# A list scheduler that models the port shared by VectorE and GpSimd, with new places for residual rows, projection weights and the first tiles, in a two-layer hybrid decoder trunk

## Chip, cores, metric

One Trainium2 chip at a time, all 8 cores (four on each of its two dies: cores 0 to 3 and 4 to 7), one sequence of the batch on each. The metric is device time in microseconds (us) of the slowest core. VectorE is written DVE, ScalarE ACT and GpSimd POOL where the profile does so; PE is TensorE and PEld its loading of weights. In profile lines L858 is line 858 of the kernel, `arena` the on-chip memory SBUF that holds all tiles, `ps` the accumulators in PSUM, `x244` a count of instructions; a group of instructions then shows busy us and the mean ns of one, and behind the bar the engine's idle time before them and what ended it.

An execution of an 8-core program is here either fast or slow. In a slow one some cores show a TensorE clock of 0.81 over part of the time and the run is some per cent longer. Only fast runs are compared, or, inside a slow run, the cores of a die whose clock was not touched.

## The reference, cut to what matters

```python
D_MODEL, BATCH, SEQ, DEPTH = 1024, 8, 4096, 2
D_FF, IN_WIDTH = 2816, 2560
# mixer A: 4 heads x 128 in chunks of 128; mixer B: 8 heads x 64, three dilated patterns

def reference(x, c, ada_w, ...):
    for l in range(DEPTH):
        mod = silu(c) @ ada_w[l] + ada_b[l]              # 9 rows of shift, scale, gate
        y = modulate(rmsnorm(h, norm_g[l, 0]), sh1, sc1)
        h = h + 0.5 * g1 * swiglu(y, ffn1_wg[l], ffn1_wu[l], ffn1_wd[l])
        y = modulate(rmsnorm(h, norm_g[l, 1]), sh2, sc2)
        u_a, v_a, q_b, k_b, v_b = split(y @ w_in[l])     # combined projection
        out_a = spatial_gating(u_a, v_a, ...)
        out_b = dilated_mixture(rope(q_b), rope(k_b), v_b)
        h = h + g2 * (concat(out_a, out_b) @ w_out[l])
        y = modulate(rmsnorm(h, norm_g[l, 2]), sh3, sc3)
        h = h + 0.5 * g3 * swiglu(y, ffn2_wg[l], ffn2_wu[l], ffn2_wd[l])
    return rmsnorm(h, final_g)
```

## The kernel before

The program is a graph of tasks. Each task names one or more engines that may do it, with a duration for each, and what it reads and writes. A list scheduler simulates the core, gives every task an engine and a place in that engine's order, and the result is emitted as instructions. A tile is 512 positions by 1024 channels; a core has eight of them. Cuts are marked `# ...`.

The scheduler. `r` is when a task can start; `m` is the later time from which TensorE may take it without risk of standing still. When several matmul chains are possible, TensorE prefers one whose `m` has passed. The other engines take the task with the smallest deadline `L`, whichever place it has in the task's list of engines.

```python
def schedule(self, bw=230.0, dlat=2300.0, dmargin=3000.0, cmargin=250.0, backlog=9000.0):
    # ...
    def release(t):
        r = m = 0.0
        if t.opts[0][0] == "pe":
            for _, ds, _, off in t.ins:
                for d in ds:
                    if d.eng == "pe":
                        continue
                    x = d.end - off
                    r = max(r, x)
                    m = max(m, x + (dmargin if d.dma else cmargin))
            # ...
        else:
            for d in t.deps:
                r = max(r, d.end)
            m = r
    # ...
    def pick(e, now):
        # ... TensorE: best by (t.mready <= now, -t.pos)
        for t in av:
            # ...
            k = t.L
            # ...
            if best is None or k < bk:
                best, bk = t, k
        return best, nxt
```

The norm of a tile and its engines, first choice first (the operation `nu` multiplies rows by the reciprocal root, `ny` applies scale and shift):

```python
def norm_sum(ht, pos):
    # ... ACT squares each of 8 row groups; they are added up
        G.op([pool(f, 1450), dve(f, 620)], reads=[ba, bq], writes=[bo], name="sqsum", pos=pos)
    # ... one matmul sums over the partitions ("nsum"), ACT: ln and exp

def norm_y(ht, slot, l, i, pos):
    # ...
        G.op([dve(f, 620), pool(f, 1450)], reads=[brs], writes=[bh], name="nu", pos=pos)
        # ...
        G.op([dve(g, 340), act(..., 705), pool(g, 1000)], reads=[bh, bm], writes=[by[kc]], name="ny", pos=pos)
```

Places: four activation slots `ACT[0..3]`, six gate-weight slots from `GU0`, three down-weight slots from `WD0`, one residual buffer `HB` that holds a whole tile for a norm, three small tiles for SwiGLU and a ring of four for residual rows:

```python
class FFN:
    def __init__(self, l, which, src, bsrc, nres=4):
        # ...
        self.res = Ring(steps(HR, 2048, nres), [128, T], F32, "hres")

def norm_load(t, src, bsrc, pos):
    ht = HT(HB)                       # always the same place
    load_h(ht, t, src, bsrc, pos)
    return ht

# start
cond(range(24), -3000.0, steps(ACT[3], 4096, 5) + steps(ACT[2], 4096, 5), WD0)   # modulation rows
for n, t in enumerate(range(4)):
    nrm(t, 0, -3000.0 + 1000.0 * n)
# ... first projection of a layer: all 20 weight blocks behind one another, from ACT[0]
mx0 = Mixer(l, ACT[0], ACT[2])
mx0.load(True, p2)
# ... end
for t in (4, 5):
    norm_out(norm_load(t, hS, bHS, s2), t, s2 + 20000.0 * (t - 4))
fc.downs((7,), ht)
norm_out(norm_load(6, hS, bHS, G.M), 6, G.M - 30000.0)
norm_out(ht, 7, G.M, True)

G.POOLS = {"ps": 8, "sg": 3}
```

The softmax here doesn't subtract the row's maximum and nothing guards it: scores larger than these inputs give would overflow.

## Time and profile before

| | before |
|---|---|
| median of 3 runs | 5174.43 us |
| the three runs | 5164.05, 5174.43 (fast), 5717.63 (slow) |
| profiled execution | slow: 5531.6 us on core 0 |
| matmuls per core | 26282 |
| busy us, core 0: PE / DVE / ACT / POOL | 5292.9 / 2923.6 / 1874.5 / 912.7 |

The busy PE of this table is stretched by the low clock, so its 96% says little about where a fast run stands still.

Every matmul got the time that it takes in an unbroken row at full clock (0.216 us for 512 columns, 0.056 or 0.05 us for the narrow ones, from the traces); they sum to 4741 us on a core. The *loss* of a stage is its length less that work. One figure is too high: the 2752 matmuls on 64 rows run in pairs, a pair every 56 ns in the trace, and 0.05 us each counts them almost twice. About 60 us of the 4741 are therefore not work (12 of them in the projection stages), the same in every kernel: differences stand, the losses themselves are too small by that much.

### The profile page before, as it was taken

The page shows a single profiled execution, that of the slowest core. Times are in us where ns is not written, and L with a number is a line of the kernel's source. Part 1 is how long each engine was busy: PE and PEld are TensorE (multiplying, and loading weights), DVE is VectorE, ACT ScalarE, POOL GpSimd, SP SyncE. Part 2 cuts the span into 40 slices and gives each one's busy share as a digit, 9 for nine tenths or more (in the row PEclk, how much of TensorE's full clock was granted, in tenths as well). Part 3 has the DMA queues.
Part 4 walks back from the last instruction along what each step waited for, and adds up shares of the span by engine and source line. Part 5 has one row for each costly group of instructions (what it writes and reads, how often), then busy time and mean ns, then how long its engine had stood idle before and what let it go on. Part 6 is the DMA issues. An engine that isn't in the chain of part 4 may idle for free.

```text
span 5531.6 us, 75923 instructions; the slowest of 8 cores (5456.8 to 5531.6 us)
## 1 busy us (share of the span) xinstructions
PE 5292.9 (96%) x26282; PEld 2385.5 (43%) x26282; DVE 2923.6 (53%) x4662; ACT 1874.5 (34%) x2715; POOL 912.7 (16%) x789
## 2 busy tenths in 40 slices
PE   3999989999999999999999999889999899999997
PEld 1344334444444444444444444344444454544443
DVE  6532387447277436445533333785554954556533
ACT  3210244435144433432122111454452544534311
POOL 2100143011143000120011001440112510012000
PEclk7788878887888888888889999999999999999998
DMA  7534756476746456565535117754756454465327
GB/s 238 145 84 112 214 154 158 107 193 184 176 161 175 123 146 182 153 207 156 159 113 190 39 39 227 191 164 129 200 143 197 152 174 149 129 183 185 115 67 253
DMA packets 389817, 866.37 MB, mean 157 GB/s; under 512 B 151456, under 2 KB 184608, under 8 KB 383264
## 3 DMA queue, kind: packets, MB, share of 16 engines
q1 hardware_dynamic: 371344, 773.02, 44.6%
q0 software_dynamic: 18096, 88.49, 10.0%
q8 instruction: 216, 3.54, 0.3%
q14 instruction: 161, 1.32, 0.1%
HBM read 760.59 MB, written 241.17 MB: 181 GB/s over the span
## 4 chain that ended last, share of the span: by engine, by line
PE 83%; DVE 7%; DMA 4%; issue 3%; ACT 2%; POOL 1%; DVEq 0%; SPq 0%; ACTq 0%; POOLq 0%
PE ps L905 46%; PE ps L932 21%; PE ps L1028 7%; PE ps L1331 4%; PE ps L1270 3%; PE ps L1247 2%; DVE arena L858 2%; DMA arena<-hS 1%; DVE arena L1088 1%; DVE arena L839 1%; DVE arena L1097 1%; DMA arena<-ada_w 1%; DMA arena<-xP 1%; DMA hS<-arena 1%; DVE arena L861 0%
## 5 line engine op out<-in xcount | busy, mean ns | idle before, releaser
L905 PE MATMUL ps<-arena 128*128 128x512 bf16 x11264 | 2783.7, 409 | 39.4 <-DVE arena L861 25.6
L905 PEld LDWEIGHTS ps<-arena 128*128 128x128 bf16 x11264 | 1135.3, 103 | 1503.7 <-issue 862.9
L932 PE MATMUL ps<-arena 128*128 128x512 bf16 x5632 | 1341.1, 403 | 14.0 <-DVE arena L936 9.3
L911 ACT ACTIVATE arena<-ps 128x512 f32<-128x512 f32 x704 | 420.0, 597 | 1483.0 <-PE ps L905 1463.0
L932 PEld LDWEIGHTS ps<-arena 128*128 128x128 bf16 x5632 | 572.5, 102 | 755.3 <-issue 356.2
L913 DVE SCALAR_TENSOR_TENSOR arena<-arena,ps 128x512 f32<-128x512 f32 x704 | 481.7, 685 | 784.9 <-ACT arena L911 783.6
L1028 PE MATMUL ps<-arena 128*128 128x512 bf16 x2560 | 643.7, 416 | 31.5 <-ACT arena L1079 10.2
L936 DVE SCALAR_TENSOR_TENSOR arena<-ps,arena 128x512 f32<-128x512 f32 x256 | 191.6, 750 | 887.0 <-PE ps L932 776.4
L918 DVE TENSOR_TENSOR arena<-ps,arena 128x512 bf16<-128x512 f32 x704 | 485.0, 690 | 277.3 <-PE ps L905 263.8
L832 ACT ACTIVATE arena<-arena 128x512 f32<-128x512 f32 x448 | 268.4, 625 | 914.4 <-DMA arena<-hS 564.5
L1253 ACT ACTIVATE arena<-ps 128x1024 bf16<-128x1024 f32 (+1 forms) x384 | 355.3, 933 | 379.6 <-PE ps L1247 379.1
L1028 PEld LDWEIGHTS ps<-arena 128*128 128x128 bf16 x2560 | 265.9, 105 | 387.2 <-issue 249.0
L839 POOL TENSOR_TENSOR arena<-arena 128x512 f32<-128x512 f32 (+1 forms) x150 | 200.7, 1338 | 993.8 <-ACT arena L832 574.9
L1256 DVE TENSOR_TENSOR arena<-arena 128x1024 bf16<-128x1024 bf16 (+1 forms) x384 | 248.7, 649 | 153.5 <-ACT arena L1253 150.8
L858 POOL TENSOR_TENSOR arena<-arena 128x512 f32<-128x512 f32 x140 | 219.8, 1588 | 387.9 <-ACT arena L846 381.1
L858 DVE TENSOR_TENSOR arena<-arena 128x512 f32<-128x512 f32 x244 | 252.7, 1076 | 28.9 <-ACT arena L846 26.7
L1331 PE MATMUL ps<-arena 128*128 128x512 bf16 x1024 | 253.2, 409 | 4.0 <-ACT arena L1110 2.2
L839 DVE TENSOR_TENSOR arena<-arena 128x512 f32<-128x512 f32 (+1 forms) x242 | 189.8, 784 | 106.7 <-ACT arena L832 73.5
L1270 PE MATMUL ps<-arena 128*128 128x128 bf16 x2736 | 225.4, 229 | 15.5 <-DVE arena L1256 14.8
L1270 PEld LDWEIGHTS ps<-arena 128*128 128x128 bf16 x2736 | 190.8, 103 | 105.8 <-issue 68.1
L1309 POOL TENSOR_TENSOR arena<-arena 64x512 bf16<-64x512 f32 x64 | 101.1, 1580 | 770.7 <-ACT arena L1304 738.9
L863 ACT ACTIVATE arena<-arena 128x512 bf16<-128x512 f32 x224 | 174.9, 808 | 141.7 <-DVE arena L858 123.5
(71 smaller groups left out, 2751.8 us busy)
## 6 DMA issues: line engine op xcount, KB each, us to landing
arena<-wguS SPq DMA_DIRECT2D x242, 512.0 KB, 4.4
arena<-hS SPq DMA_DIRECT2D x192, 512.0 KB, 6.2
arena<-wdS SPq DMA_DIRECT2D x128, 704.0 KB, 6.2
arena<-ada_w SPq DMA_DIRECT2D x144, 512.0 KB, 8.2
hS<-arena SPq DMA_DIRECT2D x248, 256.0 KB, 5.8
arena<-hS SPq DMA_DIRECT2D x184, 256.0 KB, 5.0
wguS<-wgu POOLq DMA_DIRECT2D x66, 512.0 KB, 7.5
hS<-arena SPq DMA_DIRECT2D x64, 512.0 KB, 4.9
```

The source lines that it names most:

```text
L832: G.op([act(lambda e, sq=sq, hk=hk: e.activation(out=sq, in_=hk, func=AF.Square), 520)], reads=[ht.b[kc]], writes=[bq], name="sq", pos=pos)
L839: f = lambda e, a=a, sq=sq, out=out: e.tensor_tensor(out=out, in0=a, in1=sq, op=ALU.add)
L858: f = lambda e, hk=hk: e.tensor_tensor(out=hk, in0=hk, in1=rs, op=ALU.mult)
L905: main([(lambda e, kc=kc, half=half, bk=bk, y=y, gu=gu: e.matmul(bank(bk), lhsT=gu[:, half, kc, :], rhs=y[:, kc, :], start=(kc == 0), stop ...
L911: G.op([act(lambda e, sg=sg, gb=gb: e.activation(out=sgv[sg.i], in_=bank(gb), func=AF.Tanh, scale=0.5), 490, "tanh")], reads=[gb], writes= ...
L913: G.op([dve(lambda e, sg=sg, gb=gb: e.scalar_tensor_tensor(out=sgv[sg.i], in0=sgv[sg.i], scalar=1.0, in1=bank(gb), op0=ALU.add, op1=ALU.mu ...
L918: G.op([dve(lambda e, sg=sg, ub=ub, o=o: e.tensor_tensor(out=o, in0=bank(ub), in1=sgv[sg.i], op=ALU.mult), 610)], reads=[ub, sg], writes=[ ...
L932: main([(lambda e, j=j: e.matmul(bank(bk), lhsT=wd[:, j, :], rhs=a[:, j, :], start=(j == 0), stop=(j == FC - 1)), [bwd, ba[j]], MM) for j ...
L1028: ins.append((lambda e, lhs=lhs, rhs=rhs, kc=kc: e.matmul(bank(bk), lhsT=lhs, rhs=rhs, start=(kc == 0), stop=(kc == KC - 1)), rd + [by[kc] ...
L1253: G.op([act(lambda e: e.activation(out=pv, in_=ps[:, sb.i:sb.i + 2, c0:512], func=AF.Exp, scale=0.125), 910 if anyprev else 490, "exp")], ...
L1270: return e.matmul(o, lhsT=v[:, vi, h * 64:h * 64 + 128], rhs=pT[:, h, pc, b, :], start=(pc == 0 or not prev), stop=(pc == 1))
L1331: main([(lambda e, kc=kc, m=m, bk=bk: e.matmul(bank(bk), lhsT=w[:, m, kc, :], rhs=mx[:, kc, :], start=(kc == 0), stop=(kc == KC - 1)), [bw ...
```

## The change

Its intent: let TensorE know which results are likely to be late, let the scheduler know that VectorE and GpSimd get in each other's way, give residual rows, attention reciprocals and SwiGLU tiles one common pool, put projection weights into gate slots that are free earlier, and give the first and last tiles places of their own. The core of the diff (about half left out, marked `...`; the dropped parts are the load rules, conversions and names):

```diff
-    def schedule(self, bw=230.0, dlat=2300.0, dmargin=3000.0, cmargin=250.0, backlog=9000.0):
+    def schedule(self, bw=300.0, dlat=2300.0, dmargin=3000.0, cmargin=250.0, backlog=9000.0):
...
+        port = [0.0]
...
-                        x = d.end - off
-                        r = max(r, x)
-                        m = max(m, x + (dmargin if d.dma else cmargin))
+                        r = max(r, d.end - off)
+                        m = max(m, d.late - off + cmargin)
...
                 for d in t.deps:
                     r = max(r, d.end)
-                m = r
+                    m = max(m, d.late)
...
+                if e != t.opts[0][0] and t.L > hp + 2500.0:
+                    nxt = min(nxt, now + 300.0)
+                    continue
...
+                if e == "dve" and port[0] > now and any(o[0] == e and o[3] == "x" for o in t.opts):
+                    k += 2.0 * (port[0] - now)
...
+            if e == "dve" and o[3] == "x" and free["pool"] > now and port[0] > now:
+                dur += min(port[0], free["pool"]) - now
+            if e == "pool" and not t.dma:
+                port[0] = now + dur
...
+                t.late = max(t.end, t.mready + dur + 2000.0) + dmargin
             else:
                 t.end = st + dur + LAT[e]
+                t.late = max(t.end, t.mready + o[2] + LAT[e] if e != "pe" else 0.0)
...
+        def dvex(fn, ns):
+
+            return ("dve", fn, ns, "x")
...
-                G.op([pool(f, 1450), dve(f, 620)], reads=[ba, bq], writes=[bo], name="sqsum", pos=pos)
+                G.op([pool(f, 1250), dvex(f, 615)], reads=[ba, bq], writes=[bo], name="sqsum", pos=pos)
...
-                G.op([dve(f, 620), pool(f, 1450)], reads=[brs], writes=[bh], name="nu", pos=pos)
+                G.op([dvex(f, 615), pool(f, 1300)], reads=[brs], writes=[bh], name="nu", pos=pos)
...
-                G.op([dve(g, 340), act(... 705), pool(g, 1000)],
+                G.op([act(... 725), dvex(g, 420), pool(g, 1500)],
...
-                    ap, b = self.res.take()
+                    b = Bank(1, "sm")
+                    ap = lambda: smv[b.i]
...
-        cond(range(24), -3000.0, steps(ACT[3], 4096, 5) + steps(ACT[2], 4096, 5), WD0)
+        cond(range(16), -3000.0, steps(WD0 + 4096, 4096, 3) + steps(ACT[0], 4096, 5), WD0, -26000.0)
...
-                for n, t in enumerate(range(4)):
-                    nrm(t, 0, -3000.0 + 1000.0 * n)
+                for t in range(4):
+                    nrm(t, 0, 3456.0 * t - 2500.0, None, (HB, ACT[1], ACT[2], ACT[3])[t])
...
-            mx0.load(True, p2)
+            for n, c in enumerate((1, 2, 3)):
+                mx0.load(c, GU0 + 8192 * n, True, p2)
+            for n, c in enumerate((0, 4)):
+                mx0.load(c, ACT[0] + 8192 * n, True, p2)
...
-                    norm_out(norm_load(t, hS, bHS, s2), t, s2 + 20000.0 * (t - 4))
+                    norm_out(norm_load(t, hS, bHS, s2, (GU0, HB)[t - 4]), t, s2 + 15000.0 * (t - 4))
...
-                norm_out(norm_load(6, hS, bHS, G.M), 6, G.M - 30000.0)
+                norm_out(norm_load(6, hS, bHS, G.M, GU0), 6, G.M - 25000.0)
...
-        G.POOLS = {"ps": 8, "sg": 3}
+        G.POOLS = {"ps": 8, "sm": 7}
```

An operation marked `"x"` (by `dvex`) is one on VectorE that the model lets wait until GpSimd is done. The rotary sums, the gatings, the attention normalisations and the v-norms got the same treatment as the norm lines shown.

## The prediction

> **What bounds the kernel now.** First the list of cores, because it decides how everything else is read. The profiled execution is a slow one (5533 us, while two of the three timed runs took 5164 and 5174). The clocks say why.
>
> ```profile
> core 0: 5531.6 us, clock 0.893
> core 3: 5522.7 us, clock 0.897
> ```
>
> Next the page: its engine row and the clock row of the core that it shows (core 0).
>
> ```profile
> PE 5292.9 (96%) x26282; PEld 2385.5 (43%) x26282; DVE 2923.6 (53%) x4662; ACT 1874.5 (34%) x2715; POOL 912.7 (16%) x789
> PEclk7788878887888888888889999999999999999998
> ```
>
> TensorE is busy for 96%, but up to about 2800 us its clock is 0.81. A slow TensorE hides the other engines' waits, so the idle time of that half is no measure of the fast state. Core 3 had the reverse: full clock first, 0.81 later. Both run the same program, so I joined their full-clock halves. These are busy times in stretches, core 0 first and then core 3; the number after the x is the matmuls done.
>
> ```profile
> 0.00:2815.00 2815.00, 2683.91 (x12296) 1165.43 (x12297) 1483.40 (x2395) 915.06 (x1315) 462.63 (x421) 0.81 0.58 160
> 2815.00:5532.00 2717.00, 2609.04 (x13988) 1220.08 (x13986) 1440.25 (x2267) 959.46 (x1400) 450.07 (x368) 0.98 0.51 153
> ...
> 0.00:2452.00 2452.00, 2247.30 (x12294) 1053.00 (x12295) 1474.98 (x2395) 908.62 (x1315) 464.76 (x421) 0.98 0.68 184
> ```
>
> Core 3 reaches matmul 12294 at 2452 us, core 0 at 2815. The joined execution takes 2452 + 2717 = 5169 us, which is the fast time (5164 and 5174). So I take the fast state to be this program without the 0.81 clock, and read every stage from whichever core ran it at full clock: first four rows core 3, last four core 0. Columns: stretch, its length, busy PE, PEld, DVE, ACT, POOL, clock, DMA share, GB/s.
>
> ```profile
> 0.00:160.00 160.00, 58.72 (x214) 22.34 (x215) 104.08 (x150) 61.33 (x85) 37.64 (x34) 0.84 0.77 220
> 480.00:800.00 320.00, 275.83 (x1246) 121.65 (x1245) 224.81 (x398) 127.67 (x198) 120.08 (x110) 0.95 0.72 197
> 800.00:1280.00 480.00, 457.51 (x2969) 224.22 (x2968) 292.27 (x473) 235.88 (x332) 74.32 (x66) 0.99 0.71 180
> 1280.00:1600.00 320.00, 288.73 (x1374) 130.42 (x1373) 215.80 (x387) 128.10 (x196) 127.96 (x104) 0.97 0.68 189
> ...
> 3400.00:3700.00 300.00, 263.93 (x1227) 116.94 (x1226) 225.65 (x396) 136.54 (x215) 134.05 (x114) 0.94 0.72 201
> 4150.00:4420.00 270.00, 246.90 (x1151) 111.35 (x1149) 187.65 (x346) 107.47 (x166) 109.00 (x85) 0.97 0.54 173
> 5380.00:5517.00 137.00, 119.94 (x540) 53.26 (x538) 48.47 (x64) 21.77 (x35) 9.54 (x7) 0.94 0.79 253
> 5517.00:5532.00 15.00, 0.59 (x1) 0.10 (x1) 8.86 (x14) 2.58 (x4) 0.00 (x0) 0.62 0.55 210
> ```
>
> I count a stage's loss as idle PE plus busy PE times (1 - clock), because matmuls after an idle stretch run at half clock. Start (0 to 160): 101 + 9 = 110 us. The four projection stages: 44 + 14 = 58, 31 + 9 = 40, 36 + 16 = 52 and 23 + 7 = 30, together 180. The end (from 5380): 31 + 8 = 39. The rest, mainly the attention stretches (800 to 1280 is 22 + 5 = 27), about 52. Sum 381 us. The floor that no schedule beats is therefore about 5169 - 381 = 4788 us, and the change can win only from those 381.
>
> **Why they are lost.** At the start (core 3's timeline), each of the four tiles' norms ends in a one-column-sum matmul (L842), and each waits for its own load.
>
> ```profile
> 46.67 0.59 PE L842 MATMUL ps<-arena 128*128 128x512 bf16 x1 [46.67 <-DVE arena L839]
> 75.03 0.58 PE L842 MATMUL ps<-arena 128*128 128x512 bf16 x1 [12.44 <-DVE arena L839]
> 86.26 1.44 PE L905 MATMUL ps<-arena 128*128 128x512 bf16 x3 [10.65 <-DVE arena L861]
> ```
>
> All four tiles share one residual buffer, so tile 1's load starts only at 54 us, when tile 0 is consumed. The end shows the same on core 0: a norm whose rows come late stands in front of ready matmuls.
>
> ```profile
> 5464.44 1.15 ACT L832 ACTIVATE arena<-arena 128x512 f32<-128x512 f32 x2 [18.01 <-DMA arena<-hS]
> 5475.92 0.59 PE L842 MATMUL ps<-arena 128*128 128x512 bf16 x1 [13.28 <-DVE arena L839]
> ```
>
> In the projection stages VectorE is 70 to 75% busy on average, but in bursts: counted by the program's own position marks, times the mean of each row below, 120 us of TensorE work at the first projection carry about 165 us of DVE work. Two groups are dear (core 0's groups by shape).
>
> ```profile
> L858 DVE TENSOR_TENSOR arena<-arena 128x512 f32<-128x512 f32 x244 | 252.7, 1076 | 28.9 <-ACT arena L846 26.7 <-DMA hS<-arena 2.0
> L1097 DVE TENSOR_TENSOR arena<-arena 128x512 bf16<-128x512 f32 x72 | 146.1, 2051 | 1.6 <-DVE arena L1088 1.4
> ```
>
> **What the Trainium skill says.** "SBUF - State Buffer", section "Who interferes with whom": a VectorE instruction with two SBUF inputs contends with a GpSimd instruction that reads SBUF, and whoever comes second is blocked outright. The trace agrees: of the 244 norm products (L858) on DVE, the 204 that overlapped a GpSimd operation took 1.15 us on average and the other 40 took 0.69; the SwiGLU product that reads PSUM (L913) took 0.68 either way. "TensorE: Matmul & The Clock Gate", section "What's actually happening": after an idle window of some 3.4 us the array falls to half clock, and a peak-current limiter may hold 13/16. The trace agrees on both: the clock record shows 0.50 around the stalls in stretches of 3 to 7 us, and 0.81 over half of each core's time. That page has the limiter act on a whole die; here cores 0, 1, 6 and 7 had it first and 2 to 5 later.
>
> **The change, part by part.** No arithmetic is added or removed; matmuls stay 26282. What differs is who does what, when, and where tiles lie. I compared the order of instructions of both programs on each engine.
>
> Start. Before: 16 modulation rows and 4 row loads (plus c), 21 transfers of 0.5 MB, precede the first product, which starts at 54 us; tile 1 follows only at 86. After: four tiles have four places, tile 0 and 1 load ahead of and among the 16 rows, tiles 2 and 3 right behind. That is 25 transfers before the first product, 4 more: at the roughly 320 GB/s that the DMA row shows from 11 to 44 us, 4 x 0.52 MB / 320 = 6.5 us later landing. But both norm sums are done by then, so only the modulation itself remains, and TensorE gets 32 products of two tiles, then a sum, 56 products, the last sum, and 1320 without a break (before 16, 48, 112, 1232). I put the first product at 52 to 58 us and another 8 to 12 us of gaps after it: loss 65 instead of 110, **-45 us**.
>
> Projection stages. Work leaves DVE: 46 rotary sums x 2.05 = 94 us, 86 square sums x 0.78 = 67, 69 modulations x 0.87 = 60, 23 attention normalisations x 1.04 = 24, 26 gatings x 0.84 = 22, 17 norm products x 1.08 = 18, 36 v-norms x 0.42 = 15; sum 300 us of 2924. GpSimd gets 85 + 115 + 39 + 36 + 27 - 33 - 7 = +262 us at its own means (1.85, 1.34, 1.50, 1.58, 1.59; modulations at 1.49 and v-norms at 0.71 leave it), ScalarE 91 x 0.81 + 46 x 0.48 = +96. By the position marks some 210 of the 300 us leave these four stages: the 165 us of DVE work per 120 us of TensorE become about 112. GpSimd stays at 84 of those 120 us (86 before), and rises by 27 or 28 us in each of the other three, to 138 in the busiest 180. DVE no longer exceeds TensorE, but is at 93% of it, so short waits stay. 12 of 20 projection weight loads go to gate slots and need not wait for the down products; the seven shared small tiles let residual rows be fetched earlier, which meets the 14 us that down products wait (9.3 on their residual sums). I let half of the 180 us go: **-90 us**.
>
> Attention stretches: the mask and SwiGLU orders hardly change: **-10 us**. End: tiles 4, 5 and 6 get other places than the single one, which meets the 13.3 us wait plus its cold clock and 3.1 us on a weight load; the last tile's tail (15 us after the last product) is unchanged: **-17 us**.
>
> Sum -162, so 5169 - 162 = 5007. GpSimd's longer row of work is in order and locks the port against 384 mask products and the 227 norm products left on DVE; I hold back 13 us for that: **5020 us**, 2.9% faster.
>
> **Rivals.** (a) GpSimd becomes the bound of the projection stages: it is the slowest at every operation that it gets (1.34 against 0.69), and its queue is in order. If it does, the 90 us shrink to 20 and the time is about 5090. For: the rotary sums already take 1.85 there. Against: it had 60% of those stretches free. (b) TensorE's new order waits for something else, such as the weight conversions now made in DRAM for the first down products, or loads packed more tightly; DMA is at 0.7 in these stages. Then 5080 to 5150. Against: DMA is at 0.5 or below in the gate stages where the conversions lie. (c) All losses but the start and end vanish: 4950 or less. Against: 93% DVE load leaves no room for that. (d) A fuller TensorE trips the 0.81 clock in runs that are fast now; then nothing of this shows, but such runs count as slow.
>
> **Range and chances.** The start and end (62 us) are the surest. To be over 2% faster than 5169 the time must be below 5066, that is 103 us: start, end and 41 of the 100 others. I give that 0.82, within 2% 0.16, slower 0.02. Range 4955 to 5095, from rival (c) to a little above rival (a).
>
> **What would show it.** The first long row of gate products should begin before 60 us and no gap above 8 us follow; DVE busy should fall to about 2600 to 2700 us and GpSimd rise to 1150 or more; the rotary sums on DVE should be near 26 and shorter than 2.05 us; the 13 us wait at the end gone; the losses of the four projection stages at full clock near 90. If GpSimd is above 80% busy there and matmuls wait on it, rival (a) was right; if DVE busy fell and the losses stayed, the waits were chains of latency and not load, and I was wrong in that step.

## The result, and the profile after

| | before | after |
|---|---|---|
| median, same chip | 5220.02 us (4 runs, 5164.05 to 5717.63, two of them slow) | 5043.77 us (4 runs, 5035.81 to 5560.87, one of them slow) |
| fast runs after | | 5035.81, 5041.85, 5045.69 |
| full-clock cores of all runs, mean (sd between cores) | 5153 us (11) | 5017 us (17) |

The ratio of fast runs is **0.9752** (95%: 0.9728 to 0.9775): faster, by 2.5%. Ratios here are the mean time of one kernel's fast runs over that of the other's of the same rounds, so not quite the ratio of the medians. "Full-clock cores" are all cores of all runs whose mean clock was 0.978 or more; this lets slow runs with one untouched die count too, and it is the yardstick of the experiments.

The list of cores of the kernel after. This execution is a fast one:

```profile
core 2: 5034.3 us, clock 0.987
core 6: 4988.7 us, clock 0.992
```

The page of the same execution (core 2):

```profile
PE 4797.4 (95%) x25784; PEld 2274.2 (45%) x26282; DVE 2739.8 (54%) x4359; ACT 1957.7 (39%) x2862; POOL 1147.0 (23%) x955
PEclk9999999999999999999999999999999999999999
```

The clock row (PEclk, the granted clock in tenths, in 40 slices) has no 7s and 8s any more, but that is the state of the run and not the change. (498 matmul records are missing on this core; cores 2 and 4 are therefore left out of the loss table.) DVE lost 184 busy us against the page of before, POOL gained 234, ACT 83.

The four projection stages on core 1, all at full clock (columns as in the prediction: stretch, its length, busy PE, PEld, DVE, ACT, POOL, clock, DMA share, GB/s):

```profile
522.00:837.00 315.00, 295.47 (x1586) 138.39 (x1585) 216.16 (x408) 177.06 (x275) 151.51 (x119) 0.95 0.61 167
1350.00:1608.00 258.00, 245.90 (x1439) 118.66 (x1438) 176.93 (x315) 130.53 (x193) 90.18 (x71) 0.98 0.59 170
2882.00:3296.00 414.00, 393.74 (x2035) 181.50 (x2033) 245.56 (x444) 195.56 (x303) 168.63 (x136) 0.98 0.67 188
3689.00:3968.00 279.00, 266.61 (x1314) 122.27 (x1313) 197.56 (x350) 147.02 (x224) 141.48 (x108) 0.98 0.64 193
```

DVE is busy for 836 of 1266 us, 66%. POOL is at most 51% busy (141 of 279). PE stands still for 64 us in the four.

Two groups of core 1 by shape, which answer to the dear ones of before (L858 is now L879, L1097 is L1121):

```profile
L879 DVE TENSOR_TENSOR arena<-arena 128x512 f32<-128x512 f32 x227 | 259.6, 1179 | 30.2 <-DMA hS<-arena 14.6 <-ACT arena L867 12.4 <-ACT arena L1081 3.1
L1121 POOL TENSOR_TENSOR arena<-arena 128x512 bf16<-128x512 f32 x102 | 201.4, 2055 | 85.5 <-DVE arena L1112 77.8 <-ACT arena L867 4.8 <-DMA qS<-arena 1.7
```

Of 128 rotary sums 102 are now on POOL (56 before), at 2.06 us each; the norm products left on DVE became longer, not shorter.

The start, TensorE's timeline of core 2:

```profile
46.09 0.59 PE L863 MATMUL ps<-arena 128*128 128x512 bf16 x1 [22.75 <-DVE arena L860]
62.82 10.10 PE L925 MATMUL ps<-arena 128*128 128x512 bf16 x32 [16.14 <-ACT arena L884]
74.51 0.38 PE L863 MATMUL ps<-arena 128*128 128x512 bf16 x1 [1.59 <-POOL arena L860]
```

Both norm sums are done at 47 us; then TensorE waits 16 us for the modulation (L884), and after that no gap on this core is longer than 2.5 us. Before, gaps of 12 and 11 us followed. Why the 16 us are so long, the timeline of core 1 shows:

```profile
27.09 12.24 POOL L879 TENSOR_TENSOR arena<-arena 128x512 f32<-128x512 f32 x6 [1.41 <-ACT arena L867]
29.88 2.27 DVE L756 SCALAR_TENSOR_TENSOR arena<-arena 128x1024 f32<-128x1024 f32 x1
38.15 2.27 DVE L756 SCALAR_TENSOR_TENSOR arena<-arena 128x1024 f32<-128x1024 f32 x1
40.35 1.21 DVE L756 SCALAR_TENSOR_TENSOR arena<-arena 128x1024 f32<-128x1024 f32 x1
```

L756 makes the modulation rows, L879 is the norm product. While POOL works through six norm products of tile 0 (27.09 to 39.33 us), a row takes DVE 2.27 us; the row that starts at 40.35, after them, takes 1.21. It is the same instruction on the same shape.

The end, first TensorE's timeline of core 2 and then its waits from 4900 us on:

```profile
4941.89 6.59 PE L953 MATMUL ps<-arena 128*128 128x512 bf16 x22 [3.88 <-DMA arena<-wdS]
5024.35 0.38 PE L863 MATMUL ps<-arena 128*128 128x512 bf16 x1 [3.13 <-POOL arena L860]
```

```profile
PE ps L953 <- DMA arena<-wdS: 10.2, 5, 3.9
```

The norm that stood in front of ready matmuls for 13.3 us is gone. In its place down products wait 10.2 us, in five pieces, for their own weights.

The loss by stage (us, mean of the cores at full clock with all records: 3 of the kernel before, run again in the first experiment, and 6 of the kernel after):

| stage | before | after | change | predicted |
|---|---|---|---|---|
| before the first matmul, and the first 60 us of work | 115.1 | 72.6 | -42.5 | -45 |
| four projection stages | 56.2 + 27.9 + 57.3 + 27.5 = 168.9 | 30.8 + 13.0 + 36.5 + 15.3 = 95.6 | -73.3 | -90 |
| attention, FFN and the rest | 95.5 | 71.5 | -24 | -10 |
| end (last 141 us of work) | 32.8 | 26.8 | -6.0 | -17 |
| held back | | | | +13 |
| sum | 412.2 | 266.5 | -146 | -149 |

The two cores left out of "after" are its two slowest, which makes this sum about 7 us too good (eight cores average 5014 us, these six 5008). Over all full-clock cores the mean moved from 5153 to 5017, by -136; the slowest core from 5169 to 5041, by -128, because the cores now lie further apart (sd 17 instead of 11).

### The profile page after: what moved, and what is told of

It reads as the page before. It is cut to its first block, busy times and chain, and to the rows that moved or that the text cites. A ratio compares the mean times of both kernels' runs of the same rounds, so it can differ in the third digit from the quotient of the medians.

```text
span 5034.3 us, 75361 instructions; the slowest of 8 cores (4988.7 to 5034.3 us)
## 1 busy us (share of the span) xinstructions
PE 4797.4 (95%) x25784; PEld 2274.2 (45%) x26282; DVE 2739.8 (54%) x4359; ACT 1957.7 (39%) x2862; POOL 1147.0 (23%) x955
## 3 DMA queue, kind: packets, MB, share of 16 engines
q14 instruction: 161, 1.32, 0.1%
## 4 chain that ended last, share of the span: by engine, by line
PE 77%; DMA 7%; DVE 5%; issue 4%; ACT 3%; POOL 2%; SPq 1%; DVEq 0%; POOLq 0%; ACTq 0%
PE ps L925 42%; PE ps L953 21%; PE ps L1052 6%; PE ps L1355 3%; PE ps L1293 3%; PE ps L1270 2%; DMA hS<-arena 2%; DMA arena<-hS 1%; DMA arena<-ada_w 1%; DVE arena L1112 1%; POOL arena L1121 1%; DVE arena L879 1%; DMA arena<-wdS 1%; DVE arena L860 1%; DMA vS<-arena 1%
## 5 line engine op out<-in xcount | busy, mean ns | idle before, releaser
L925 PE MATMUL ps<-arena 128*128 128x512 bf16 x10957 | 2486.5, 381 | 54.6 <-ACT arena L884 16.8
L925 PEld LDWEIGHTS ps<-arena 128*128 128x128 bf16 x11264 | 1077.4, 98 | 1308.4 <-issue 59.2
L953 PE MATMUL ps<-arena 128*128 128x512 bf16 x5501 | 1228.0, 380 | 19.8 <-DMA arena<-wdS 10.2
L953 PEld LDWEIGHTS ps<-arena 128*128 128x128 bf16 x5632 | 547.3, 98 | 673.2 <-issue 23.8
L1052 PE MATMUL ps<-arena 128*128 128x512 bf16 x2528 | 575.7, 386 | 21.8 <-DVE arena L1112 6.2
L860 POOL TENSOR_TENSOR arena<-arena 128x512 f32<-128x512 f32 (+1 forms) x236 | 316.0, 1339 | 1066.2 <-ACT arena L853 987.7
L1052 PEld LDWEIGHTS ps<-arena 128*128 128x128 bf16 x2560 | 253.0, 99 | 333.4 <-issue 45.5
L1279 DVE TENSOR_TENSOR arena<-arena 128x1024 bf16<-128x1024 bf16 (+1 forms) x384 | 261.9, 684 | 154.9 <-ACT arena L1276 151.6
L879 POOL TENSOR_TENSOR arena<-arena 128x512 f32<-128x512 f32 x157 | 262.6, 1697 | 206.2 <-ACT arena L867 165.6
L884 ACT ACTIVATE arena<-arena 128x512 bf16<-128x512 f32 x315 | 242.4, 806 | 99.0 <-DVE arena L879 53.9
L879 DVE TENSOR_TENSOR arena<-arena 128x512 f32<-128x512 f32 x227 | 257.9, 1172 | 29.6 <-DMA hS<-arena 12.7
L1333 POOL TENSOR_TENSOR arena<-arena 64x512 bf16<-64x512 f32 x87 | 125.1, 1440 | 611.5 <-ACT arena L1328 560.7
L756 DVE SCALAR_TENSOR_TENSOR arena<-arena 128x1024 f32<-128x1024 f32 x144 | 196.3, 1369 | 68.2 <-DMA arena<-ada_w 68.0
L1355 PE MATMUL ps<-arena 128*128 128x512 bf16 x1000 | 231.5, 387 | 1.9 <-issue 0.8
L1293 PE MATMUL ps<-arena 128*128 128x128 bf16 x2736 | 212.6, 220 | 15.5 <-DVE arena L1279 10.1
L1293 PEld LDWEIGHTS ps<-arena 128*128 128x128 bf16 x2736 | 180.8, 98 | 101.0 <-issue 25.6
```

Of the source, the lines that this page charges most:

```text
L860: f = lambda e, a=a, sq=sq, out=out: e.tensor_tensor(out=out, in0=a, in1=sq, op=ALU.add)
L879: f = lambda e, hk=hk: e.tensor_tensor(out=hk, in0=hk, in1=rs, op=ALU.mult)
L925: main([(lambda e, kc=kc, half=half, bk=bk, y=y, gu=gu: e.matmul(bank(bk), lhsT=gu[:, half, kc, :], rhs=y[:, kc, :], start=(kc == 0), stop ...
L953: main([(lambda e, j=j: e.matmul(bank(bk), lhsT=wd[:, j, :], rhs=a[:, j, :], start=(j == 0), stop=(j == FC - 1)), [bwd, ba[j]], MM) for j ...
L1052: ins.append((lambda e, lhs=lhs, rhs=rhs, kc=kc: e.matmul(bank(bk), lhsT=lhs, rhs=rhs, start=(kc == 0), stop=(kc == KC - 1)), rd + [by[kc] ...
L1293: return e.matmul(o, lhsT=v[:, vi, h * 64:h * 64 + 128], rhs=pT[:, h, pc, b, :], start=(pc == 0 or not prev), stop=(pc == 1))
```

## The experiments

Each kernel is the kernel after with one part undone, unless it says otherwise. All twelve gave correct results. The yardstick is the mean of the full-clock cores: **before 5153, after 5017**. Two fair measures of its noise: cores of one kernel differ by an sd of 10 to 22 us, and stages that an edit does not touch moved by up to 5 us (the first attention stretch by up to 10), since any edit reshuffles the whole schedule. A difference of less than about 15 us is therefore not called shown. The experiments ran on three chips, with the kernel before beside them each time (its full-clock cores averaged 5156, 5152 and 5152 us); the kernel after was not run again, so differences to its 5017 may be between chips.

### 1. Is the joined reading true? The kernel before, unchanged

> The kernel before, unchanged, for a profile in the fast state. The reading of the prediction is that the fast state has no 0.81 clock at all: then this profile shows clocks of 1.00 and 0.50 only, a span of 5155 to 5180 us, and losses by stage (idle TensorE plus half-clock matmuls) like those joined from two cores: 110 to 115 us at the start, about 50 in the first projection stage, some 425 us in all over the bare matmul work of 4741. Rival: the fast state has the 0.81 clock too, for a shorter time, and its losses are smaller than the joined ones; then a mean clock of about 0.96 shows.

All three runs were slow, by one die. The list of cores of its profiled execution, the two medians:

```profile
die 0 (median of its cores): 5156.3 us, clock 0.979
die 1 (median of its cores): 5406.5 us, clock 0.920
```

The slowest core of die 0 took 5168.2 us without any 0.81 in its clock record: the 5169 us joined from two halves in the prediction was right to a microsecond, and fast runs are this program without the 0.81 clock (fast profiles of experiments 7 to 9 hold 3 to 30 us of it on some cores). Its own losses (412 us) replace the 381 that I had counted from the joined halves. So the prediction's floor "that no schedule beats", 4788 us, was too high: by this count it is 4741, and about 4680 with the pairs counted once.

### 2. The start alone

```diff
-cond(range(16), -3000.0, steps(WD0 + 4096, 4096, 3) + steps(ACT[0], 4096, 5), WD0, -26000.0)
+cond(range(24), -3000.0, steps(ACT[3], 4096, 5) + steps(ACT[2], 4096, 5), WD0)
-    nrm(t, 0, 3456.0 * t - 2500.0, None, (HB, ACT[1], ACT[2], ACT[3])[t])
+    nrm(t, 0, 1000.0 * t - 3000.0)
```

(and the later modulation rows at their old places, and four small loads of constants without their early due date)

> The changed kernel with the start of the kernel before (24 modulation rows first, one residual place for all four tiles). If the start's gain is its own, the time rises by the 41 us that the two traces differ up to the first 60 us of matmul work: 5075 to 5090 us against about 5041. Rival: what is won at the start is given back later, because the tiles' norms and the later modulation rows only move; then it stays within 15 us of 5041.

One of four runs was fast, 5099.57 us; the mean full-clock core is 5059, 42 more than after. The loss before and in the first 60 us of work is 94.3 instead of 72.6, and that of the first FFN stage 23.1 instead of 7.2: together 38 of the 42. That 42 is also what the start gained (-42.5) is a coincidence. In the stage itself these lines bring back only 21.7 us; the other 16 appear in the stage behind it, which lost just 11.9 in the kernel before. With the old lines the start still loses 21 us less than before (94.3 against 115.1). Experiment 4, which has the engine part with the old start, gains nothing there, so this half comes from a part never undone by itself (the transfer rate, the load rules or the due dates). Which one is not shown.

### 3. The choice of engines and the port, all undone

```diff
-    return ("dve", fn, ns, "x")
+    return ("dve", fn, ns, None)
-    if e != t.opts[0][0] and t.L > hp + 2500.0:
-        nxt = min(nxt, now + 300.0)
-        continue
-G.op([pool(f, 1250), dvex(f, 615)], ... name="sqsum")
+G.op([pool(f, 1450), dve(f, 620)], ... name="sqsum")
 # and likewise the old order and durations of nu, ny, vnorm, ropeadd, oamul, anorm
```

> The changed kernel with the engine choice of the kernel before: old order of engines for norms, rotary sums, gatings and v-norms, old durations, no port in the scheduler's model. If relieved DVE is what helps the projection stages, their losses return (first stage from 31 to about 50 us, the other three by 16, 23 and 10) and the time rises by 50 to 75 us to 5090 to 5115. Rival: weight loads in gate slots, shared small tiles and late transfers did it; then the time rises by less than 20 us. A second rival, that the move to GpSimd costs as much in port waits as it saves, lets it stay the same or fall.

Three fast runs: 5163.94, 5166.92, 5167.48 us; mean core 5144, +127 and more than expected. Without this part nearly the whole gain is gone, although the start keeps 36 of its 42.5 us: other stages lose what it wins. The four projection stages lose 182.4 us, more than in the kernel before (168.9): the rest of the change alone does not help there.

### 4. The same part alone, on the kernel before

```diff
 # the kernel before, and of the change nothing but this:
+        def dvex(fn, ns):
+            return ("dve", fn, ns, "x")
-G.op([pool(f, 1450), dve(f, 620)], ... name="sqsum")
+G.op([pool(f, 1250), dvex(f, 615)], ... name="sqsum")
 # and the new lists of nu, ny, vnorm, ropeadd, oamul, anorm; dvex for fin, adarow, mask;
 # port[0] in the scheduler; a second choice only when it is urgent (t.L > hp + 2500.0 waits)
```

> The kernel before with the engine part of the change alone (order of engines, durations, the port in the scheduler's model, a second choice only when urgent). Undoing this part in the changed kernel cost about 130 us, more than half of what the four projection stages and the start explain, so if it is the cause on its own, it brings the projection stages from 169 us of loss to about 95 and the attention stretches down by 15 to 20 here too: 5060 to 5085 us, mean of the full-clock cores 5050 to 5075. Rival: the parts need each other (new tile places make room for the moved work); then it stays above 5115.

Fast runs 5080.17 and 5084.11 us, mean core 5067: 86 less than before. Projection stages 108.4 instead of 168.9, the two attention stretches 34.1 instead of 62.4, start unchanged (114.5). Forwards 86 and backwards 127 differ, so parts of the change interact; but both say that this is the largest part.

### 5. The port alone

```diff
 def dvex(fn, ns):
-    return ("dve", fn, ns, "x")
+    return ("dve", fn, ns, None)
```

One word: the lists of engines and durations stay new, but no operation is marked, so the scheduler neither waits for the port nor lengthens anything.

> The changed kernel with its order of engines and durations, but without the port in the scheduler's model (no operation is marked as sharing it). The scheduler then puts more on DVE again (norm products 280 on DVE against 227, rotary sums 48 against 26). If the preference order is what counts, the time stays within 20 us of 5041; if the modelled port is, most of the 125 us that undoing the whole engine part cost come back: 5110 or more. I expect something between: mean of the full-clock cores 5050 to 5080, with the losses in the projection stages.

Fast at 5134.07 us (a run at 5191.18 also counted as fast, with its cores at a slightly lower clock), mean core 5121: +103, against the 5050 to 5080 that I expected. So 103 of the 127 us of experiment 3 hang on the port in the model, and only some 24 on the lists and the urgency rule. I had taken the lists for at least half.

What the model does with it is seen in the groups of core 1 (compare with the L879 line of the kernel after above):

```profile
L879 DVE TENSOR_TENSOR arena<-arena 128x512 f32<-128x512 f32 x280 | 278.3, 1027 | 30.0 <-DMA hS<-arena 15.7 <-ACT arena L867 14.1
```

Blind to the port, the scheduler believes that DVE does these in 615 ns and gives it 280 of them; with the port it gives 227. Rotary sums on DVE are 48 instead of 26, modulations 70 instead of 30. The port model thus does not make an operation on DVE cheaper (1027 ns without it, 1179 with it). It moves operations away, and it may give TensorE an order that fits better what DVE really delivers; the two were not told apart. A simpler rival was not tried either: a fixed longer duration for these operations on DVE, which would also push them away.

Five kernels side by side, the first projection stage of each layer on core 1, cut at the same work (440 to 720 and 2700 to 3080 us of it). Before, in the run of experiment 1:

```profile
566.00:900.00 334.00, 298.29 (x1569) 137.14 (x1568) 258.56 (x463) 158.32 (x242) 111.41 (x103) 0.94 0.65 175
2964.00:3403.00 439.00, 397.97 (x2036) 182.24 (x2034) 287.07 (x501) 170.62 (x266) 140.77 (x124) 0.97 0.69 187
```

All of the engine part undone (experiment 3):

```profile
533.00:859.00 326.00, 294.24 (x1588) 138.04 (x1587) 245.12 (x447) 167.85 (x253) 130.91 (x105) 0.95 0.59 161
2949.00:3385.00 436.00, 399.07 (x2031) 183.43 (x2030) 280.21 (x488) 182.66 (x275) 146.46 (x121) 0.95 0.64 178
```

Only the port off:

```profile
523.00:851.00 328.00, 295.39 (x1586) 137.43 (x1584) 237.87 (x431) 177.83 (x277) 120.97 (x94) 0.95 0.59 160
2931.00:3362.00 431.00, 395.90 (x2035) 182.76 (x2034) 266.32 (x470) 193.57 (x303) 136.20 (x110) 0.96 0.66 180
```

The kernel before with the engine part alone (experiment 4):

```profile
566.00:879.00 313.00, 290.15 (x1573) 134.83 (x1572) 226.50 (x406) 179.93 (x283) 153.62 (x125) 0.98 0.72 181
2926.00:3350.00 424.00, 395.93 (x2044) 181.60 (x2042) 257.71 (x443) 199.75 (x313) 170.99 (x141) 0.97 0.71 196
```

Read the lengths against busy DVE (third busy column) and busy POOL (fifth). The kernels with the port in the model have the least DVE work (216 and 227 in the first stage, against 238 to 259), the *most* POOL work (152 and 154, against 111 to 131), and the shortest stages (315 and 313, against 326 to 334). The second stage gives the same order. That POOL would become the bound is refuted: more POOL work goes with less loss.

TensorE's own waits name the engine. On core 1, summed over the four projection stages, its waits on DVE are 73 us before, 74 in experiment 3, 83 with only the port off, 42 with the engine part alone and 25 in the kernel after. Its waits on ACT are 27 to 36 us in all five, those on POOL 1 to 9.

### 6. The projection weights' places

```diff
-for n, c in enumerate((1, 2, 3)):
-    mx0.load(c, GU0 + 8192 * n, True, p2)
-for n, c in enumerate((0, 4)):
-    mx0.load(c, ACT[0] + 8192 * n, True, p2)
+for c in (1, 2, 3, 0, 4):
+    mx0.load(c, ACT[0] + 8192 * c, True, p2)
```

> The changed kernel with all five projection weight pieces in the activations' slots, as before. If the early loads matter, the first projection stage of each layer starts with a wait for weights: 5 to 20 us per layer, 10 to 40 us in all. If they do not (in the trace of the kernel before no matmul waits for a w_in load), the time stays within 10 us of 5041. I expect the second.

One fast run, 5078.52 us, mean core 5054 (+37), where I had expected less than 10. The profiled execution fell in the slow state on both dies, so it could not show where. The same kernel was therefore run once more:

> The kernel with the projection weights back in the activations' slots once more, for a profile with a full clock: its full-clock cores were 37 us slower on average than the changed kernel's, against my expectation of less than 10, and its first profile was slow on both dies. If late weights are the cause, matmuls of the first projection wait for w_in loads or the weights' issue; if the slots are, the first gate products after the projection wait, because their activation slots hold projection weights until its end; if it is only another schedule, the loss spreads over all stages by a few us each.

Fast at 5071.47 us, mean core 5047 (+30). The loss lies where these weights are used: first projection stage of layer one 43.9 instead of 30.8, of layer two 46.6 instead of 36.5; the second projection stages, which the edit leaves alone, 14.4 and 16.8 instead of 13.0 and 15.3. Which wait carries it is less clear. The waits of core 1 in the first of these stages (524 to 856 us):

```profile
PE ps L1052 <- ACT arena L1134: 7.7, 3, 4.2
PE ps L953 <- DVE arena L957: 4.0, 2, 2.4
```

L1052 is the projection, L953 the down product. They wait for ACT and for the residual sums; in the whole list of this stage nothing waits for a projection weight. Over the four projection stages of core 1, waits on ACT are 44 us against 29 in the kernel after, those on DVE 26 against 25. So the places are worth some 30 us (shown twice), and the loss stands in waits on ACT; that it comes about through the order which the scheduler finds, and not through a late load, is only inferred, and why ACT is late stays open.

### 7. One pool against two

```diff
-b = Bank(1, "sm");  ap = lambda: smv[b.i]
+b = Bank(1, "rs");  ap = lambda: smv[3 + b.i]
-G.POOLS = {"ps": 8, "sm": 7}
+G.POOLS = {"ps": 8, "sm": 3, "rs": 4}
```

(and reciprocals of the attention in "rs"; a load may take the last free place of its pool, which the kernel after forbids)

> The changed kernel with two pools of small tiles instead of the shared seven: three for the SwiGLU gates, four for residual rows and the attention's reciprocals. In the kernel before, down products waited 12 to 14 us for residual sums and loads. If the shared pool removed that, the time rises by 5 to 15 us; if four places for residual rows are enough, nothing beyond 10 us of scheduling noise changes. I expect the second.

Fast at 5046.70, 5052.78 and 5054.01 us, mean core 5029: +11. The first FFN lost 7.7 us more and the second 5.2 more, which is where residual rows are fetched, but as a whole the step is below what I call shown. It is small at best.

### 8. Handing lateness on

```diff
-    m = max(m, d.late - off + cmargin)
+    m = max(m, d.end - off + (dmargin if d.dma else cmargin))
-    m = max(m, d.late)
+    m = r
```

(and the old margin of 1 us for soft dependencies)

> The changed kernel with the old margins for lateness (3 us for a transfer, 0.25 us for another engine, nothing handed on from a late transfer to what depends on it). Only TensorE's choice between ready products uses this. If it guards against real lateness, matmuls wait more for norms and loads: +10 to +30 us, most of it in the projection stages and the first product's neighbourhood. Rival: it is only a tie break, and the time stays within 10 us of 5041 (mean of the full-clock cores 5014). I expect the second by a little.

Fast at 5022.56, 5025.20 and 5025.24 us, mean core 5003: 14 *less* than after. The part that I named first when I stated the intent brings nothing here, and may cost a little. The difference is at the edge of the noise of any reshuffled schedule.

### 9. The start without the collision

Only for tiles 0 and 1 the norm product may go to DVE alone, so that POOL does not hold the modulation rows:

```diff
-G.op([dvex(f, 615), pool(f, 1300)], ... name="nu")
+G.op([dvex(f, 615)] if first else [dvex(f, 615), pool(f, 1300)], ... name="nu")
```

> The changed kernel with the norm products of the first two tiles on DVE alone. In the changed kernel's trace ten modulation rows at the start took 2.27 us instead of 1.22 while GpSimd held norm products, and the first gate product came at 63.6 us. If the port is the cause, rows fall back to 1.22 us, DVE gets 10 x 1.05 us back and spends 9 x 0.69 more, and the first product comes at 55 to 60 us, total 3 to 8 us less. Rival: the rows' own loads bound the start (they end at about 46 us plus latency), and the first product stays at 62 or later.

TensorE's timeline of core 6, the slowest:

```profile
58.42 0.58 PE L925 MATMUL ps<-arena 128*128 128x512 bf16 x1 [13.26 <-ACT arena L884]
```

The first product comes at 58.4 us instead of 62.2 on the same core (58.0 to 61.4 on all eight, 62.2 to 63.6 in the kernel after), and the modulation rows of cores 1 and 6 take 1.21 to 1.32 us again, all but one or two of 16. So the collision did delay it. But the loss of the start falls only from 72.6 to 69.3 us, and the mean core is 5012 (-5, not shown; fast runs 5036.08, 5041.91, 5058.79). What begins earlier does not have the following tiles ready earlier.

### 10. The end

```diff
-norm_out(norm_load(t, hS, bHS, s2, (GU0, HB)[t - 4]), t, s2 + 15000.0 * (t - 4))
+norm_out(norm_load(t, hS, bHS, s2), t, s2 + 20000.0 * (t - 4))
-norm_out(norm_load(6, hS, bHS, G.M, GU0), 6, G.M - 25000.0)
+norm_out(norm_load(6, hS, bHS, G.M), 6, G.M - 30000.0)
```

> The changed kernel with the last tiles' norms all in the one place, as before. I predicted 17 us for the end and the traces show 6: the 13 us wait for the rows of tile 5 went, but down products now wait some 10 us for their weights (wdS), 3 before. If that is right, this brings the 13 us wait back and takes most of the weight waits away: +3 to +10 us. Rival: the weight waits are there anyway, then +13 us or more.

Fast at 5044.05, 5046.09 and 5049.63 us, mean core 5024 (+7); the ratio to before, 0.9743 (0.9708 to 0.9778), is flattered by some runs of before with short dips of the clock (fast ones up to 5191 us). The end itself loses 30.6 instead of 26.8. TensorE's waits from 4900 us on, core 2:

```profile
PE ps L953 <- DMA arena<-wdS: 6.2, 3, 2.6
PE ps L863 <- DVE arena L860: 3.8, 1, 3.8
```

With the old places the norm waits 3.8 us for DVE (and 4.2 for POOL, against 3.1 in the kernel after), and the weights 6.2 instead of 10.2. Cores differ, though: over the six with all records the weights take 5.5 to 7.9 us here and 5.2 to 15.0 in the kernel after. The 13.3 us wait does not return even with one place for all: it had already gone with the rest of the schedule. The separate places seem to trade a norm's wait for waits on weights, and the stage's loss differs by some 4 us, which is no more than noise.

### 11. A better version: lateness not handed on, and the start without the collision

The edits of 8 and 9 together.

> The changed kernel without handing on lateness and with the norm products of the first two tiles on DVE alone. Without lateness the full-clock cores took 5003 us on average against 5017, with the DVE norm products 5012. If both add up: mean 4995 to 5002, slowest core 5015 to 5025. Rival: both were noise of the schedule; then about 5040 again.

Fast at 5016.26, 5020.44 and 5021.16 us of eight runs, ratio to before **0.9691** (0.9656 to 0.9725). It has the same runs of before below it as experiment 10, so the core means are the fairer figure: 5004, which is 0.971 of 5153; the kernel after is at 0.974. By its fast runs it is the quickest kernel seen (5019 on average, against 5041 for the kernel after). Over the kernel before the gain is shown; over the kernel after, the 13 us of the core means are below what I call shown. It equals experiment 8 alone (5003), so the start edit adds nothing here.

## Why the prediction was right, and where its steps were not

5020 us was predicted, 4955 to 5095 as the range; the fast runs gave 5036 to 5046. "Faster by over 2%" came true at 2.5%. That the sum came so near (-146 against -149 in the table) is partly luck: the projection stages and the end gave 17 and 11 us less than said, the attention and the rest 14 more.

**The joined reading of a slow profile: right** (experiment 1).

**Start, -45: right in size** (-42.5), wrong in one detail. The order of loads and norms read from the finished program was right; the lines that place the tiles bring only half of it in that stage (experiment 2). The first product came at 62.8 us and not at 52 to 58. I had added four row loads at the DMA's speed and nothing for the port, though I had quoted the collision myself. Modulation rows took 2.27 us instead of 1.21 while POOL ran norm products. The skill page that I cited ("SBUF — State Buffer", "Who interferes with whom") is borne out by it. The gaps afterwards were shorter than the 8 to 12 us allowed, which made up for it.

**Projection stages, -90: right mechanism, a fifth too large** (-73). TensorE's waits on DVE fell there from 73 to 25 us, as DVE was relieved. The estimate moved 300 us of work off DVE at the durations of before, 210 of them in these stages. Busy DVE fell by 173 only (core 1, 2917 to 2744), in these stages by 120 (956 to 836). Against core 1 of experiment 1, four groups left on DVE became longer: norm products 1092 to 1179 ns (x227), masks of two blocks 693 to 743 (x304), modulation rows 1234 to 1355 (x144), square sums 771 to 958 (x125). That is 20 + 15 + 17 + 23 = 75 us that POOL's longer work gave back, of the 127 missing; the rest I did not trace. I had held back 13 us for just this; in busy time it was 75. DVE busy was to end at 2600 to 2700 us and ended at 2740, POOL at 1150 or more and ended at 1147. (DVE's load in these stages before was 67 to 75%, not the 70 to 75 of the prediction.) The rotary sums on DVE are 26, as read from the order, but 1.88 us long on core 1, still far from the 0.65 us that the scheduler's table assumes.

**Which part carries it: not asked.** The prediction read the moved counts from the finished orders and did not ask which lines of the change move them. Before experiment 5 I still took the lists of engines for at least half; it shows that most comes from the port in the model (+103 when off).

**Attention, FFN, rest, -10: too small** (-24). The first attention stretch alone gave 14, the other 5. Experiment 4 puts this down to the engine part too: 62.4 to 34.1 us with that part alone. I had left the mask products there as they were; that their collision with POOL is what was won is not shown, since they became longer (693 to 743 ns).

**End, -17: the step that failed in size** (-6). "Tiles 4, 5 and 6 get other places than the single one, which meets the 13.3 us wait plus its cold clock and 3.1 us on a weight load": the norm's wait went, but the wait on weight loads grew from 3.1 to 10.2 us. And in experiment 10 the stage loses only about 4 us more with the old places, not 13; the rest of the wait went with something else.

**The rivals.** (a) POOL as the bound: refuted, it is at most 51% busy, and all waits of TensorE on it come to some 13 us on cores 1 and 2, none longer than 3.1. (b) New waits on loads: true in small, 10.2 us at the end and 6.5 us in the projection stages of core 1, where there were none before. (c) 4950 or less: no, 95.6 us stay in the projection stages, in short waits. (d) Slow runs occur in every kernel that was run more than once, and are not compared. The prediction's remark that the 0.81 clock did not act on a whole die ("cores 0, 1, 6 and 7 had it first and 2 to 5 later") reads each core's own time as a common one, which the traces don't have; see the last section.

**What stays open.** Why ACT is late without the new weight places; which part brings the other half of the start's gain; what the new bandwidth figure, the load rules and the due dates do, which were never undone by themselves; and why parts do not add: undone one by one on the kernel after they are worth 127, 42, 30, 11, 7 and -14 us, together 203, where the whole is 136.

## What to carry to other kernels

If a scheduler shares work between two engines that block each other, put the blocking into its model before tuning lists of engines: here taking out that one word cost 103 of the 136 us, and more work on the slower engine went with a faster kernel, since the engine that TensorE waits for was left freer (its waits on DVE in the projection stages fell from 73 to 25 us). When you move work next to an engine, re-price the work that stays, since its durations will change too. And judge a gain by the stage in which it should appear: a wait that disappears at a named place may have gone for another reason, and may come back as a wait on the next thing in the row.

## What the Trainium skill lacked or had wrong

- "TensorE: Matmul & The Clock Gate" (Part 1; the limiter stands under "Seeing it yourself", not in the section that the prediction names) says that the 13/16 clock comes over the whole die within 5 to 20 us of a third core's dense matmuls and stays while the load lasts. Nothing here shows that wrong. Fast runs have next to no 0.81, but no trace shows that more than two cores of a die ran at once in them, for each core's times count from its own start. In every die with much 0.81, one pair of cores has it from its first matmuls on and the other pair up to its end: in the profile of before cores 0 and 1 from 62 to 2872 us and cores 2 and 3 from 2856 to 5513; in experiment 1 cores 6 and 7 from 64 to 2031 and cores 4 and 5 from 3596 to 5404. That is what the rule gives if the two pairs start apart and overlap in part, by an estimate from these figures 2856 - 62 = 2.8 ms apart in the first case. Without a common clock it is not shown; what the page lacks is this: how far apart the cores of one program may start, which would decide whether a run is fast or slow.
- "Perfetto Trace Analysis" ("Optimizing Scalar/DVE Operations") says that offloading between VectorE and GpSimd might not help because of their common port. That is a caution and no error, but with the port in the scheduler's model it did help: together with moves to ScalarE 5153 to 5067 us on its own, POOL's busy time in the first projection stage rising from 111 to 154 us. Taken out of the model of the kernel after, with the same lists of engines, it left 5121 instead of 5017 us.
- "SBUF — State Buffer" ("Who interferes with whom") is right about the blocking, but gives no size for two rows of work that meet. Here they took turns, one modulation row and one norm product every 2.20 us (rows start at 29.88, 32.08 and 34.28 us on core 1): the row takes 2.27 us instead of 1.21, the norm product on POOL 2.24, where the fastest in the trace takes 1.25.
